# A 31-tap depthwise convolution moved to column tiles of TensorE, and the 256-token x operand laid out in gapless rows at another offset

## The chip, the cores and the metric

The kernel runs on one core of one Trainium2 chip. A core has TensorE (PE, with the weight loads listed apart as PEld), VectorE (DVE), ScalarE (ACT), GpSimd (POOL) and SyncE (SP, which here only issues loads). The metric is the device time of one execution in microseconds (us); lower is better.

## The reference, cut to what matters

Two stacked blocks of layers for one sequence of 256 tokens with model width 1024, all in float32. The first block has four layers (mixers: retention, convolution, dilated attention, retention), each followed by a gated feed-forward layer (hidden 2816); the second puts 16 meta tokens ahead of the 256 (272 tokens) and has a mixer with two branches, a feed-forward layer of 4096, a differential attention and another feed-forward layer. The mixer that the change rewrites is the convolution, layer 1:

```
def _conv_mixer(h, w_in, b_in, w_dw, b_dw, ln_g, ln_b, w_out, b_out):
    a = h @ w_in + b_in
    u = a[..., :D_MODEL] * jax.nn.sigmoid(a[..., D_MODEL:])
    u = lax.conv_general_dilated(              # 31 taps, each channel by itself
        u, w_dw[:, None, :], window_strides=(1,), padding=[(15, 15)],
        dimension_numbers=('NWC', 'WIO', 'NWC'), feature_group_count=D_MODEL) + b_dw
    u = jax.nn.silu(_layernorm(u, ln_g, ln_b))
    return u @ w_out + b_out
```

## The kernel before, in words

Activations lie channels on partitions, tokens along the row: 8 chunks (KD) of 128 channels by 256 tokens (S), or 272 (T2) in the second block. Every float32 value that a large product uses is split in two float32r parts, high and low. The normed input of a layer is the pair `xh`, `xl` (written by `prenorm_chunk`), the hidden of a layer are the pairs `hh`, `hl`, and weights come in quads of 8 blocks of 128x128: SP loads two quads at a time (`raw`, 1 MB), ACT casts the high part (`hi`, 128x1024), DVE subtracts the low part (`lo`). `mmB` (line 322) is one block: three matmuls, hi by xh, hi by xl, lo by xh, with the weights stationary and 256 (or 272) tokens moving. `mmA` (line 331) is the other way round for values that are wanted with tokens on partitions: x is stationary, 512 columns of hi or lo move. `xk` and `xtok` (lines 613 and 616) give the operand slices of x; `kouter` opens a layer with the contraction chunk outside, so that PE can follow chunk by chunk while the norm is still being written.

There is no scheduler behind the kernel: a planner inside it (`Kern.now`, `Engine.cost`, generators in `bg` that `pump` steps between blocks) fixes the order of every queue when the kernel is built, by estimated costs; on the chip each engine runs its queue in that order and waits on semaphores.

The convolution (`conv`, line 1058): 128 blocks of `conv_w_in` give 8 pairs of channel chunks (value and gate); `evac` makes U[c], 128 channels by 256 tokens with 15 zeros at either side. The 31 taps of a chunk are shared out by `TAPS`: the first 13 to 16 go to PE (`taps_pe`: ACT scales the identity by the tap's weights into a 128x128 diagonal `cdg`, and a float32 matmul of U shifted by the tap is accumulated), 121 over all chunks; the other 127 go to DVE (`taps_dve`: scalar_tensor_tensor on 128x256 into two accumulators `cv` and `cacc`). `combine` adds the PE sum to the DVE sum, `stats` builds the layer norm's sums, `act` normalises, and `conv_w_out` follows.

By the allocation of the built program, addresses along a partition are: xh at byte 27392 with 1088 bytes from chunk to chunk, xl at 36096, hi buffers from 72992 in steps of 4096, lo buffers from 101664 in steps of 4096 (a block is 512 bytes); the hh and hl that 256-token products read lie 1024 bytes apart, the first at 136672. Counted from the start of a weight block and modulo 512: xh and xl of chunk k at 480 + 64k, hh and hl at 192, the same for all of them.

Of the kernel before, what the change touches and what calls it, by code (L numbers as in the profile page):

```python
# [19 lines left out]
D = 1024  # L20
# [15 lines left out]
def _vec_layout():  # L36
    n = 0
    for i in range(4):
        for j in range(4):
            VEC[f"n{i}{j}"] = n  # L40
            n += 8
    for name, w in (
        ("mix0", 8), ("mix1", 8), ("mlp0", 8), ("mlp1", 8), ("fin", 8),
        ("cb_in", 16), ("cb_dw", 8), ("cln_g", 8), ("cln_b", 8), ("cb_out", 8),
        ("lconv_w", 32), ("lconv_b", 8), ("lb_r", 8), ("lb_i", 8), ("lam", 8),
        ("mnorm", 8), ("subln", 1), ("cw_dw", 248),
    ):
        VEC[name] = n
        n += w
    return n  # L50
# [13 lines left out]
def shape_consts():  # L64
# [23 lines left out]
    c["amask"] = mk  # L88
    c["cmask"] = np.where(s[None, :] <= s[:, None], 0.0, BIG).astype(f)
# [21 lines left out]
LRU_B = 4  # L111

# [90 lines left out]
class Kern:  # L203
# [212 lines left out]
    def setup(self):  # L416
# [3 lines left out]
        self.xh = cp.tile([128, KD, T2], F32R, name="xh")  # L420
        self.xl = cp.tile([128, KD, T2], F32R, name="xl")
# [142 lines left out]
    def prenorm_chunk(self, c, src, gain, T, perm, have=False):  # L564
# [3 lines left out]
        h, l = view(self.xh[:, c, :T]), view(self.xl[:, c, :T])  # L568
# [54 lines left out]
    def kouter(self, T, outs, key, cut=lambda n: 0):  # L623


        for k in range(KD):
            self.feed(2)
            if k == 0:
                ws = []
                for n, (b, o, first) in enumerate(outs):  # L630
                    w = self.blk(*key(0, n))
                    ws.append(w)
                    self.mm(b[:, o:o + T - cut(n)], w[0], self.xh[:, 0, cut(n):T], first, False)
                for n, (b, o, first) in enumerate(outs):
                    self.mm(b[:, o:o + T - cut(n)], ws[n][1], self.xh[:, 0, cut(n):T], False, False)
                for n, (b, o, first) in enumerate(outs):
                    self.mm(b[:, o:o + T - cut(n)], ws[n][0], self.xl[:, 0, cut(n):T], False, False)
            else:
                for n, (b, o, first) in enumerate(outs):
                    self.mmB(b[:, o:o + T - cut(n)], self.blk(*key(k, n)), self.xtok(k, cut(n), T - cut(n)),  # L640
                             False, k == KD - 1)
# [95 lines left out]
    def boundary(self, perm, gain2, perm2=False, full=False):  # L737
# [39 lines left out]
        if first:  # L777
            self.ve.tensor_tensor(mg, mg, ps[:, :S], ALU.mult)
            o = T - S
            self.ve.tensor_tensor(self.xh[:, 0, o:T], mg, xg, ALU.add)  # L780
            if o:
                self.ve.tensor_scalar(self.xh[:, 0, :o], self.X[:, 0, :o], g, None, ALU.mult)
# [271 lines left out]

    TAPS = (16, 13, 14, 16, 16, 16, 16, 14)
    CD = 1.0

    def conv(self, i, j):
# [8 lines left out]
        ln, U, sums = {}, {}, {}  # L1067
# [5 lines left out]
        def evac(c, b):  # L1073
# [3 lines left out]
            u = self.wk.tile([128, S + 30], F32, name="U", tag="U", bufs=8)  # L1077
# [13 lines left out]
            U[c] = u  # L1091

        def claim():

            for c in range(KD):
                while c not in U:
                    yield None
                for k in range(self.TAPS[c]):
                    d = self.wk.tile([128, 128], F32, name="cdg", tag="cdg", bufs=8)
                    self.sc.activation(d, self.ident, AF.Copy, scale=self.vec("cw_dw", 8 * k + c))  # L1100
                    yield c, k, d

        def taps_pe():
            src, ahead, b = claim(), deque(), None
            more = True
            while more or ahead:
                while more and len(ahead) < 4:
                    x = next(src, 0)
                    if x is None:
                        break  # L1110
                    if x == 0:
                        more = False
                    else:
                        ahead.append(x)
                if not ahead:
                    yield 0.3
                    continue
                c, k, d = ahead.popleft()
                last = k == self.TAPS[c] - 1
                if k == 0:  # L1120
                    b, = yield from self.need(1)
                yield self.w(d, U[c])
                self.mm(b[:, :S], d, U[c][:, k:k + S], k == 0, last)
                if last:
                    sums[c] = b
                    self.spawn(combine(c))
                if k % 2:
                    yield 0.0

        def taps_dve():  # L1130
            for c in range(KD):
                while c not in U:
                    yield 0.3
                shifted = "shift" in done
                if shifted:
                    done.add(("shifted", c))
                acc = [cv[:, c], self.wk.tile([128, S], F32, name="cacc", tag="cacc")]
                for n, k in enumerate(range(self.TAPS[c], 31)):
                    w = self.vec("cw_dw", 8 * k + c)
                    x, a = U[c][:, k:k + S], acc[n % 2]  # L1140
                    if n == 0 and shifted:
                        self.ve.scalar_tensor_tensor(out=a, in0=x, scalar=w, in1=K, op0=ALU.mult, op1=ALU.subtract)
                    elif n == 1 and not shifted:
                        self.ve.tensor_scalar(a, x, w, None, ALU.mult)
                    elif n < 2:
                        self.ve.tensor_scalar(a, x, w, self.vec("cb_dw", c), ALU.mult, ALU.add)
                    else:
                        self.ve.scalar_tensor_tensor(out=a, in0=x, scalar=w, in1=a, op0=ALU.mult, op1=ALU.add)
                    yield self.ve.clock - self.now - 0.5
                self.ve.tensor_tensor(acc[0], acc[0], acc[1], ALU.add)  # L1150
                done.add(c)

        def combine(c):
            while c not in done:
                yield 0.1
            b = sums[c]
            yield self.w(b, cv[:, c]) + (0.0 if c == KD - 1 else self.CD)
            self.ve.tensor_tensor(cv[:, c], cv[:, c], b[:, :S], ALU.add)
# [94 lines left out]
        self.spawn(taps_pe())  # L1253
        self.spawn(taps_dve())
        self.spawn(stats())
        for c in range(3, KD):
# [4 lines left out]
            self.spawn(evac(c, p))  # L1261
        self.until(lambda: len(yk) > 0)
# [613 lines left out]
    def diff(self):  # L1876
# [44 lines left out]
        def project(n):  # L1921
            p = self.bank()
            o = cut(n[0])
            for k in range(KD):
                self.mmB(p[:, :T2 - o], self.blk(*w_in(k, n)), self.xtok(k, o, T2 - o), k == 0, k == KD - 1)
# [169 lines left out]
def pack(inputs):  # L2095
# [20 lines left out]
    for a, b in (("cb_in", "conv_b_in"), ("cb_dw", "conv_b_dw"), ("cln_g", "conv_ln_g"), ("cln_b", "conv_ln_b"),  # L2116
                 ("cb_out", "conv_b_out"), ("cw_dw", "conv_w_dw"), ("lconv_w", "lru_conv_w_2"),
# [3 lines left out]
    c["vec"] = v  # L2121
    row = np.concatenate([f["ret_log1m_decay"].reshape(-1), f["ab_if_bias_2"][0], f["c_lambda_2"][0].reshape(-1)])
# [43 lines left out]
```

## Time and profile before

| | |
|---|---|
| median of 3 runs | 2404.72 us (2403.23 to 2404.73) |
| profiled execution, device time | 2403.58 us |
| its span (first to last instruction) | 2401.7 us |
| PE busy | 2352.9 us, 98% |
| PEld busy | 2242.4 us, 93% |
| DVE busy | 1651.1 us, 69% |
| ACT busy | 1161.6 us, 48% |
| POOL busy | 222.3 us, 9% |

The profile is of one execution. Matmuls are pipelined: the duration of one in the profile reaches past the start of the next, so what a matmul costs in a stream is read from the distance between starts. A float32 matmul (not float32r, and not a transposition by the identity) leaves two records.

### The profile page before, as it was taken

The numbers are of one execution on the slowest core, as the hardware profiler recorded it, in microseconds if no ns is written. First come the engines' busy times: TensorE is split into PE (matmuls) and PEld (weight loads), VectorE is DVE, ScalarE is ACT, GpSimd is POOL, SyncE is SP. The second block draws the span as 40 slices with busy tenths as digits, with TensorE's granted clock in tenths as the row PEclk, the third lists the DMA queues.
The fourth block names the chain that finished last, engine by engine and source line by source line (L and its number), as shares of the span: only waits on it lengthen the run. The fifth ranks groups of instructions, "written<-read, shape, count | busy, mean of one in ns | idle before, by whom it ended". The sixth has DMA issues, their size and how long they took to land.

```text
span 2401.7 us, 43737 instructions
## 1 busy us (share of the span) xinstructions
PE 2352.9 (98%) x18193; PEld 2242.4 (93%) x18193; DVE 1651.1 (69%) x2826; ACT 1161.6 (48%) x1879; POOL 222.3 (9%) x284
## 2 busy tenths in 40 slices
PE   7999999999999999999999999999999999999998
PEld 7889999989998989999998899999999999989998
DVE  7556865898667768876676658566766756586764
ACT  5544544565444454454445444445655434356543
POOL 1002000112002000020020002002000100132000
PEclk9999999999999999999999999999999999999999
DMA  6443553304553544335544444554433445433552
GB/s 237 171 169 131 211 193 141 141 24 155 208 185 137 193 150 141 141 141 193 193 147 182 171 160 172 184 192 159 141 141 139 160 163 190 162 115 114 211 194 106
DMA packets 56935, 387.89 MB, mean 162 GB/s; under 512 B 7360, under 2 KB 8128, under 8 KB 10656
## 3 DMA queue, kind: packets, MB, share of 16 engines
q1 hardware_dynamic: 53280, 381.18, 44.1%
q10 hardware_dynamic: 3200, 2.99, 0.4%
q8 instruction: 143, 2.34, 0.4%
q0 software_dynamic: 256, 0.92, 0.1%
q14 instruction: 56, 0.46, 0.1%
HBM read 384.02 MB, written 1.05 MB: 160 GB/s over the span
## 4 chain that ended last, share of the span: by engine, by line
PE 86%; DVE 6%; POOL 3%; issue 2%; ACT 2%; DMA 1%; SPq 0%; ACTq 0%; DVEq 0%; POOLq 0%
PE b L312 84%; PE b L316 2%; DVE lo L198 2%; POOL X L198 1%; ACT hi L198 1%; POOL acc L198 1%; DVE cv L198 1%; DVE xl L198 1%; DVE cacc L198 1%; POOL rs L198 1%; DVE xh L198 0%; PE b L345 0%; DVE psq L198 0%; DMA raw<-in_w 0%; POOL psq L198 0%
## 5 line engine op out<-in xcount | busy, mean ns | idle before, releaser
L198 DVE TENSOR_TENSOR lo<-raw,hi 128x1024 fp32r<-128x1024 f32 (+1 forms) x723 | 876.7, 1235 | 266.4 <-ACT hi L198 264.8
L312 PE MATMUL b<-xh,hi 128*128 128x256 f32 (+1 forms) x3272 | 937.3, 290 | 14.2 <-ACT hi L198 9.3
L312 PE MATMUL b<-xl,hi 128*128 128x256 f32 (+1 forms) x3272 | 917.3, 284 | 4.3 <-DVE xl L198 4.1
L312 PE MATMUL b<-xh,lo 128*128 128x256 f32 (+1 forms) x3272 | 914.1, 283 | 0.9 <-DVE lo L198 0.9
L198 ACT CAST hi<-raw 128x1024 fp32r<-128x1024 f32 (+1 forms) x723 | 738.5, 1044 | 266.4 <-PE b L312 227.0
L312 PEld LDWEIGHTS b<-xh,hi 128*128 128x128 f32 x3272 | 611.9, 189 | 23.6 <-ACT hi L198 9.5
L312 PEld LDWEIGHTS b<-xl,hi 128*128 128x128 f32 x3272 | 611.8, 188 | 8.9 <-DVE xl L198 6.7
L312 PEld LDWEIGHTS b<-xh,lo 128*128 128x128 f32 x3272 | 614.2, 189 | 1.1 <-DVE lo L198 1.1
L312 PE MATMUL b<-hh,hi 128*128 128x256 f32 (+1 forms) x1792 | 504.1, 281 | 0.6 <-ACT hh L198 0.6
L312 PE MATMUL b<-hl,hi 128*128 128x256 f32 (+1 forms) x1792 | 500.2, 279 | 0.6 <-DVE hl L198 0.4
L312 PE MATMUL b<-hh,lo 128*128 128x256 f32 (+1 forms) x1792 | 500.3, 279 | 0.0
L312 PEld LDWEIGHTS b<-hh,hi 128*128 128x128 f32 x1792 | 336.9, 188 | 2.3 <-issue 0.8
L312 PEld LDWEIGHTS b<-hl,hi 128*128 128x128 f32 x1792 | 336.8, 188 | 2.0 <-DVE hl L198 1.6
L312 PEld LDWEIGHTS b<-hh,lo 128*128 128x128 f32 x1792 | 336.9, 188 | 0.0
L198 DVE TENSOR_TENSOR t<-b,R 128x512 f32<-128x512 f32 x96 | 65.4, 689 | 199.3 <-PE b L312 197.5
L312 PE MATMUL b<-hi,xh 128*128 128x512 f32 x352 | 142.4, 404 | 0.5 <-DVE xh L198 0.5
L312 PE MATMUL b<-lo,xh 128*128 128x512 f32 x352 | 140.0, 398 | 0.3 <-DVE lo L198 0.3
L312 PE MATMUL b<-hi,xl 128*128 128x512 f32 x352 | 139.3, 396 | 0.0
L198 ACT ACTIVATE sg<-t 128x256 f32<-128x256 f32 x88 | 36.6, 419 | 193.3 <-DVE t L198 193.2
L198 POOL TENSOR_TENSOR acc<-acc,sq 128x256 f32<-128x256 f32 (+1 forms) x90 | 83.1, 923 | 385.5 <-ACT sq L198 233.0
L198 POOL TENSOR_TENSOR psq<-psq 128x512 f32<-128x512 f32 x8 | 12.0, 1506 | 973.8 <-ACT psq L198 973.8
L198 ACT ACTIVATE sq<-X 128x256 f32<-128x256 f32 (+1 forms) x91 | 39.7, 439 | 116.8 <-POOL X L198 73.4
(313 smaller groups left out, 2127.9 us busy)
## 6 DMA issues: line engine op xcount, KB each, us to landing
raw<-in_w SPq DMA_DIRECT2D x359, 1024.0 KB, 4.8
raw<-in_w SPq DMA_DIRECT2D x4, 256.0 KB, 6.0
raw<-in_w SPq DMA_DIRECT2D x2, 512.0 KB, 9.7
dp<-in_c_dp SPq DMA_DIRECT2D x2, 512.0 KB, 4.8
wr<-in_lru_w SPq DMA_DIRECT2D x1, 1024.0 KB, 6.8
X<-in_x POOLq DMA_DIRECT2D x1, 640.0 KB, 9.5
c_rcs<-in_c_rcs ACTq DMA_DIRECT2D x2, 256.0 KB, 5.0
c_amask<-in_c_amask ACTq DMA_DIRECT2D x1, 512.0 KB, 3.5
```

The source lines that it names most:

```text
L198: return f(*args, **kw)
L312: self.nc.tensor.matmul(out, lhsT, rhs, start=start, stop=stop, skip_group_check=True)
L316: self.nc.tensor.transpose(out, in_, ident)
```

## The change

Three things are edited. First, the x operand: `xh` and `xl` become flat tiles. A 256-token layer keeps chunk k at element 56 + 256k (bytes 224 + 1024k), a 272-token layer at 272k as before. With `cw_dw` gone from the vector table all that is allocated behind it moves down by 992 bytes together: xh starts at 26400, hi at 72000, hh at 135680. Counted from the start of a weight block and modulo 512, xh and xl of a 256-token layer now lie at 192 for every k; hh and hl stay at 192; the 272-token layout stays where it was against the weights. The differential attention's queries (256 tokens cut out of 272) keep the 272-token layout.

Second, the taps: all 31 (and a 32nd of weight zero) go to PE, and `taps_dve`, `TAPS` and the 121 diagonals are gone. After U[c] is written, ACT's queue issues four DMAs within SBUF that lay each group g of 32 channels out on 128 partitions, 4 shifts of each channel (`cr`, line 1108 of the changed file). POOL multiplies a 32-column selection matrix by the tap weights (`ctw`, 128x1024). Then a chunk is 32 float32 matmuls: 8 steps of 4 taps by 4 channel groups, each with 128 rows, 32 weight columns and 256 tokens, writing 32 PSUM partitions, the four groups in turn.

Third, the order: the taps of chunks 5 and 6 wait in the plan until all of `conv_w_in` is issued, so that they stand ahead of chunk 7's. `combine` only adds the bias (ACT, or DVE with the shift).

```
+    XOFF = 56
+    def xpart(self, t, k, T, t0=0, n=None):
+        a = (self.XOFF if T == S else 0) + k * T + t0
+        return t[:, a:a + (T - t0 if n is None else n)]
     def xk(self, k, T):
-        return self.xh[:, k, :T], self.xl[:, k, :T]
-    def xtok(self, k, t0, n):
-        return self.xh[:, k, t0:t0 + n], self.xl[:, k, t0:t0 + n]
+        return self.xtok(k, 0, T, T)
+    def xtok(self, k, t0, n, T=S):
+        return self.xpart(self.xh, k, T, t0, n), self.xpart(self.xl, k, T, t0, n)
...
-    TAPS = (16, 13, 14, 16, 16, 16, 16, 14)
-    CD = 1.0
+    COPY, TAP = 4.0, 3.5
...
             self.unlock("evac")
-            U[c] = u
+            r = self.wk.tile([128, 4, RW], F32, name="cr", tag="cr", bufs=3)
+            yield self.w(u) - 0.3
+            x = u[:]
+            ps = x.ap[0][0]
+            for g in range(4):
+                nc.scalar.dma_start(out=r[:, g], in_=bass.AP(x.tensor, x.offset + 32 * g * ps, [[ps, 32], [1, 4], [1, RW]]))
+            self.times.write(r, max(self.now, self.times.read(u)) + self.COPY)
+            U[c] = r
...
+        def tapw(c):
+            w = self.wk.tile([128, 32, 32], F32, name="ctw", tag="ctw", bufs=3)
+            self.gp.tensor_tensor(w, m32[:, None, :].to_broadcast([128, 32, 32]),
+                                  cwt[:, 32 * c:32 * c + 32].unsqueeze(2).to_broadcast([128, 32, 32]), ALU.mult)
+            return w
+        def taps():
+            ws = {c: tapw(c) for c in range(2)}
             for c in range(KD):
+                while c not in U or c in (KD - 3, KD - 2) and "in" not in done:
                     yield 0.3
+                yield self.w(U[c], ws[c])
+                b, = yield from self.need(1)
+                w = ws.pop(c)
+                for q in range(8):
+                    for g in range(4):
+                        self.mm(b[32 * g:32 * g + 32, :S], w[:, 4 * q + g], U[c][:, g, 4 * q:4 * q + S], q == 0, q == 7,
+                                TAP / 32)
+                if c + 2 < KD:
+                    ws[c + 2] = tapw(c + 2)
+                self.spawn(combine(c, b))
+                yield 0.0
+        def combine(c, b):
+            yield self.w(b)
+            if "shift" in done:
+                done.add(("shifted", c))
+                self.ve.scalar_tensor_tensor(out=cv[:, c], in0=b[:, :S], scalar=self.vec("cb_dw", c), in1=K,
+                                             op0=ALU.add, op1=ALU.subtract)
+            else:
+                self.sc.activation(cv[:, c], b[:, :S], AF.Identity, bias=self.vec("cb_dw", c))
             self.rel(b)
...
-        self.spawn(taps_pe())
-        self.spawn(taps_dve())
+        self.spawn(taps())
         self.spawn(stats())
```

On PE at the end of the convolution's first product the order before was this (`b<-xh,hi` and its like are blocks of `conv_w_in`, `U,cdg` a tap by a diagonal, the `onesD` rows the layer norm's sums, the `hi` rows matmuls that fill a wait, `hh` the first of `conv_w_out`):

```order
L312 MATMUL b_5188<-U,cdg 128x256 x2
L312 MATMUL b_5353<-U,cdg 128x256 x16
L312 MATMUL b_5425<-U,cdg 128x256 x16
L312 MATMUL b_5497<-U,cdg 128x256 x16
L312 MATMUL b_5569<-U,cdg 128x256 x16
L312 MATMUL b_5640<-U,cdg 128x256 x10
L312 MATMUL b_5683<-onesD,a_5267 128x1 x2
L312 MATMUL b_5683<-onesD,a_5268 128x1 x2
L312 MATMUL b_5640<-U,cdg 128x256 x4
L312 MATMUL b_5683<-onesD,cv 128x1 x2
```

Of the 121 taps 41 stood among the blocks ahead of these rows and 80 stand here, in the order of chunks 2 to 7. The same place on PE in the changed kernel:

```order
L316 MATMUL b_5309<-xh,lo 128x256
L316 MATMUL b_5387<-cr,ctw 32x256 x32
L316 MATMUL b_5429<-cr,ctw 32x256 x32
L316 MATMUL b_5468<-cr,ctw 32x256 x32
L316 MATMUL b_5505<-onesD,a_5203 128x1 x2
L316 MATMUL b_5505<-onesD,a_5204 128x1 x2
L316 MATMUL b_5505<-onesD,cv 128x1 x2
```

Three chunks (5, 6, 7) are left behind the blocks, 32 matmuls each; the other five stand among the blocks in groups of 32.

On ACT's queue in the changed kernel, at the same place (`sg` is the gate's sigmoid, `cr<-U` the four DMA issues of a chunk, `cv<-b` a chunk's combine, `csq` the squares for the norm):

```order
L202 ACTIVATE sg<-t_5317,V 128x256
L202 CAST hi<-raw 128x1024
L1110 DMA cr<-U 128x1x284 x4
L202 ACTIVATE sg<-t_5381,V 128x256
L1110 DMA cr<-U 128x1x284 x4
L202 ACTIVATE csq<-cv 128x256 x3
L202 ACT_TABLE_LOAD
```

Chunk 7's four issues come right behind its sigmoid and wait for DVE's U; nothing but the squares and the norm's table load is queued behind them.

## Rows read from the trace of the kernel before

**Rows 1.** The page: busy times, and the chain that ended last by engine.
```profile
PE 2352.9 (98%) x18193; PEld 2242.4 (93%) x18193; DVE 1651.1 (69%) x2826; ACT 1161.6 (48%) x1879; POOL 222.3 (9%) x284
...
PE 86%; DVE 6%; POOL 3%; issue 2%; ACT 2%; DMA 1%; SPq 0%; ACTq 0%; DVEq 0%; POOLq 0%
```

**Rows 2.** Groups of PE by form: count, busy us, mean ns, idle before, releasers.
```profile
L312 PE MATMUL b<-xh,hi 128*128 128x256 f32 x2496 | 708.2, 287 | 13.0 <-ACT hi L198 9.3 <-DVE xh L198 3.2
...
L312 PE MATMUL b<-hh,hi 128*128 128x256 f32 x1408 | 391.8, 278 | 0.0
...
L312 PE MATMUL b<-hi,xh 128*128 128x512 f32 x352 | 142.4, 404 | 0.5 <-DVE xh L198 0.5
```

**Rows 3.** Timeline of PE, layer 0's feed-forward: start us, us, what.
```profile
301.05 0.28 PE L312 MATMUL b<-xh,hi 128*128 128x256 f32 x1
...
306.74 0.28 PE L312 MATMUL b<-hh,hi 128*128 128x256 f32 x1
...
309.46 0.28 PE L312 MATMUL b<-xh,hi 128*128 128x256 f32 x1
```

**Rows 4.** Timeline of PE in a 272-token feed-forward layer.
```profile
1944.13 0.29 PE L312 MATMUL b<-hh,hi 128*128 128x272 f32 x1
...
1989.53 0.29 PE L312 MATMUL b<-xh,hi 128*128 128x272 f32 x1
...
2031.62 0.29 PE L312 MATMUL b<-hh,hi 128*128 128x272 f32 x1
```

**Rows 5.** Timeline of PE in layer 0's retention, 512 columns moving.
```profile
47.84 0.39 PE L312 MATMUL b<-lo,xh 128*128 128x512 f32 x1
...
60.19 0.39 PE L312 MATMUL b<-hi,xh 128*128 128x512 f32 x1
...
63.69 0.39 PE L312 MATMUL b<-vg,ah 128*128 128x512 f32 x1
...
65.50 0.40 PE L312 MATMUL b<-vg,al 128*128 128x512 f32 x1
```

**Rows 6.** What reads tile U: durations min/median/max, first and last start us.
```profile
L312 PE MATMUL b<-U,cdg x242: 377/378/631, 444.3 to 525.4; 128*128 128x256 f32 x121
L198 DVE SCALAR_TENSOR_TENSOR cv<-U,V,cv x59: 469/475/955, 448.3 to 524.6; 128x256 f32<-128x256 f32 x59
```

**Rows 7.** Convolution by stretch: length; busy PE, PEld, DVE, ACT, POOL; PEclk; DMA.
```profile
414.60:485.40 70.80, 67.28 (x487) 63.77 (x488) 63.34 (x117) 40.59 (x85) 16.57 (x33) 1.00 0.36 129
485.40:526.60 41.20, 38.09 (x171) 31.39 (x169) 40.41 (x92) 23.92 (x79) 8.54 (x10) 0.96 0.02 10
```

**Rows 8.** Timeline of DVE just behind the convolution's first product.
```profile
486.46 0.68 DVE L198 TENSOR_TENSOR t<-b,R 128x512 f32<-128x512 f32 x1
...
488.57 0.48 DVE L198 SCALAR_TENSOR_TENSOR U<-t,V,sg 128x256 f32<-128x256 f32 x1
```

**Rows 9.** Timeline of ACT with its queue's DMA issues (ACTq), two places.
```profile
10.96 0.45 ACTq L413 DMA_DIRECT2D c_ident<-in_c_ident  x1
...
487.18 0.51 ACT L198 ACTIVATE sg<-t,V 128x256 f32<-128x256 f32 x1 [2.34 <-DVE t L198]
```

**Rows 10.** DMA issues by line: count, KB each, median us from issue to landing.
```profile
raw<-in_w SPq DMA_DIRECT2D x359, 1024.0 KB, 4.8
...
out<-fo ACTq DMA_DIRECT2D x2, 256.0 KB, 2.5
```

**Rows 11.** Timeline of PE: float32 matmuls on the whole array and on tiles.
```profile
45.88 1.89 PE L312 MATMUL b<-qk 128*128 128x256 f32 x8
...
831.22 0.28 PE L312 MATMUL b<-xh,lo 128*128 128x256 f32 x1
831.43 1.09 PE L312 MATMUL b<-as,av 128*64 128x128 f32 x16
...
1720.72 1.58 PE L312 MATMUL b<-vt,A 128*16 128x258 f32 x6
```

**Rows 12.** Timeline of POOL in the convolution.
```profile
489.93 0.84 POOL L198 TENSOR_TENSOR a<-a,cv 128x256 f32<-128x256 f32 x1 [7.13 <-DVE cv L198]
```

More of the change, by code (lines that the diff above doesn't have):

```diff
@@ L45, in _vec_layout @@
         ("lconv_w", 32), ("lconv_b", 8), ("lb_r", 8), ("lb_i", 8), ("lam", 8),
-        ("mnorm", 8), ("subln", 1), ("cw_dw", 248),
+        ("mnorm", 8), ("subln", 1),
     ):
@@ L88, in shape_consts @@
     c["amask"] = mk
+    c["m32"] = (s[:, None] // 4 == np.arange(32)[None, :]).astype(f)
     c["cmask"] = np.where(s[None, :] <= s[:, None], 0.0, BIG).astype(f)
@@ L111 @@
 LRU_B = 4
+UW, RW = S + 31, S + 28
 class Bank:
@@ L419, in setup @@
         self.V = cp.tile([128, NV], F32, name="V")
-        self.xh = cp.tile([128, KD, T2], F32R, name="xh")
-        self.xl = cp.tile([128, KD, T2], F32R, name="xl")
+        self.xh = cp.tile([128, KD * T2], F32R, name="xh")
+        self.xl = cp.tile([128, KD * T2], F32R, name="xl")
         self.R = cp.tile([128, T2], F32, name="R")
@@ L567, in prenorm_chunk @@
         view = (lambda a: a.rearrange("p (j i a) -> p j i a", j=4, i=4)) if perm else (lambda a: a)
-        h, l = view(self.xh[:, c, :T]), view(self.xl[:, c, :T])
+        h, l = [view(x) for x in self.xk(c, T)]
         g = self.vec(gain, c)
@@ L779, in boundary @@
             o = T - S
-            self.ve.tensor_tensor(self.xh[:, 0, o:T], mg, xg, ALU.add)
+            self.ve.tensor_tensor(self.xpart(self.xh, 0, T, o), mg, xg, ALU.add)
             if o:
-                self.ve.tensor_scalar(self.xh[:, 0, :o], self.X[:, 0, :o], g, None, ALU.mult)
+                self.ve.tensor_scalar(self.xpart(self.xh, 0, T, 0, o), self.X[:, 0, :o], g, None, ALU.mult)
         self.feeder = feed()
@@ L1066, in conv @@
         self.ve.memset(self.ones256, 1.0 / 256)
-        ln, U, sums = {}, {}, {}
+        m32 = self.const("m32")
+        cwt = self.w1.tile([128, 256], F32, name="cwt")
+        nc.scalar.dma_start(out=cwt, in_=self.ap["cwt"])
+        ln, U = {}, {}
         done = set()
@@ L1076, in evac @@
             t = self.wk.tile([128, 2, S], F32, name="t1", tag="t1")
-            u = self.wk.tile([128, S + 30], F32, name="U", tag="U", bufs=8)
+            u = self.wk.tile([128, UW], F32, name="U", tag="U", bufs=3)
             self.gp.memset(u[:, 0:15], 0.0)
@@ L1090, in evac @@
             self.unlock("evac")
-            U[c] = u
-        def claim():
-            for c in range(KD):
[L1096 to L1115, printed above, removed]
-                    yield 0.3
[L1117 to L1158, printed above, removed]
+            r = self.wk.tile([128, 4, RW], F32, name="cr", tag="cr", bufs=3)
[4 more added lines that the diff above has]
+                nc.scalar.dma_start(out=r[:, g], in_=bass.AP(x.tensor, x.offset + 32 * g * ps, [[ps, 32], [1, 4], [1, RW]]))
@@ L1261, in conv @@
             self.spawn(evac(c, p))
+        done.add("in")
         self.until(lambda: len(yk) > 0)
@@ L1924, in project @@
             for k in range(KD):
[L1925 removed]
+                self.mmB(p[:, :T2 - o], self.blk(*w_in(k, n)), self.xtok(k, o, T2 - o, T2), k == 0, k == KD - 1)
             keep(n, p)
@@ L2121, in pack @@
     c["vec"] = v
+    w = np.zeros((32, D), np.float32)
+    w[:31] = f["conv_w_dw"][0]
+    c["cwt"] = np.ascontiguousarray(w.reshape(8, 4, 8, 4, 32).transpose(4, 1, 2, 0, 3).reshape(128, 256))
     row = np.concatenate([f["ret_log1m_decay"].reshape(-1), f["ab_if_bias_2"][0], f["c_lambda_2"][0].reshape(-1)])
```

11 lines of the change are left out of this document (6 added, 5 removed).

## The prediction, made before the changed kernel was run

> **What bounds the kernel now.** I read the page first: PE is busy 98% of the span and the chain that ended last is 86% PE [rows 1]. So what counts is how fast PE goes from one matmul to the next, and where it has to follow another engine.
>
> For the first I took the groups of PE by form [rows 2]: a 256-column matmul is listed at 278 to 287 ns, but these durations overlap, so the cost is the distance between starts. In the timeline of a feed-forward layer 48 matmuls with x moving stand between 301.05 and 306.74, which is 118.5 ns each, and the 24 with hh or hl moving that follow stand between 306.74 and 309.46, 113.3 ns each [rows 3]. Same columns, weights out of the same buffers, microseconds apart; x costs 5.2 ns more. Two things differ: where x lies against the weights (480 + 64k modulo 512, against a constant 192), and what the matmuls belong to.
>
> For the second I took the convolution by stretch [rows 7]. While `conv_w_in` runs, PE is busy 67.28 of 70.80 us. In the next 41.20 us PE works at taps, but DVE is busy 40.41 of them: 127 of the 248 taps are DVE's and the last starts at 524.6 [rows 6]. That stretch ends when DVE does.
>
> **The x operand.** Rows 2 count 2496 blocks of three 256-column matmuls. Of these, 64 blocks are the differential attention's queries, which keep the old layout; 2432 blocks, 7296 matmuls, move to 192, where hh and hl are. If place decides, each falls from 118.5 to 113.3 ns: 7296 x 5.2 = 37.9 us. At the front of a layer PE waits for x chunks and weights, 13.0 us before the first of a block's three [rows 2]; those waits end when they ended, so some faster blocks only wait longer. I take 2 us off: **36 us**. The ends are 0 (place is not the cause) and 38.
>
> The 1056 matmuls with 512 columns moving (three times the 352 of rows 2) have x as weights. They take (60.19 - 47.84) / 53 = 233 ns; the retention's own, whose operands are at 0 modulo 512 to each other, take (65.50 - 63.69) / 8 = 226 ns [rows 5]. After the change these stand at 320, which no row shows. Between 2 us lost and 1056 x 6.7 ns = 7 us won I take **3 us**, nearer the lower end, since at 272 columns place does not tell: 360 matmuls with hh and hl at all multiples of 64 take 126.1 ns, 336 with x 125.3 [rows 4]. Those 272-column matmuls keep their place and their time.
>
> **The taps.** A float32 matmul of 256 columns on the whole array is two records 216 ns apart, (1.89 - 0.38) / 7, so 0.43 us [rows 11]. Removed are 121 of them: 41 among the blocks (17.7 us) and 80 in the second stretch. Added are 256, each a quarter of the array's columns. Were they to run one by one, a chunk would cost 32 x 0.43 = 13.8 us; four at once, 3.45 us. The nearest row is `as,av`: 64 columns wide, alternating halves, 8 matmuls of 128 columns in 16 records, (1.09 - 0.32) / 7 = 110 ns for one against 216 ns on the whole array, so two halves run at once [rows 11]. Narrowness alone wins nothing: `vt,A`, 16 columns wide and always at one place, takes 240 ns a record [rows 11]. I take four at once, carrying on what the halves do, and keep two at once (6.9 us) and one (13.8 us) as bounds. Going onto tiles costs 0.09 us (the start at 831.43 stands 0.21 behind one that is followed at 0.118 elsewhere) and a first record longer by 0.05; I put 0.23 us to a visit and assume the way back like the way in.
>
> The Trainium skill, "TensorE: Matmul & The Clock Gate", Part 3 (Measured speedup vs the span model), gives 2.38 times for three column tiles of 32. Carried to four as an estimate, 3.2 times, a chunk would be 4.3 us and the kernel 7 us slower than I say; no row here has more than two tiles.
>
> Among the blocks: five groups, 5 x (3.45 + 0.23) = 18.4 us for 17.7, **0.7 us lost**. Behind the blocks: three groups, 10.4 + 0.25 us, then a drain and one DVE pass of some 0.5 us, 11.4 us in place of 41.2: **29.8 us won**. Together 29 us.
>
> **What covers the copies.** Chunk 7 cannot start before its U is made and copied. Its evacuation took from 486.46 to 489.05 between DVE taps that are now gone [rows 8]; by the durations 0.68, 0.51 and 0.48 us it takes some 2.1 us from the last block [rows 8, 9]. Four issues of 0.45 us on ACT follow [rows 9], and a landing, for which the nearest row is the 256 KB that ACT's queue sends in 2.5 us [rows 10]: 6.4 us. Chunks 5 and 6 cover 7.1 us, so it is hidden with 0.7 us to spare; at the 4.8 us of a weight load [rows 10] PE would wait 1.6 us. The earlier chunks have blocks between. Behind the issues ACT has weight casts, which run some four quads ahead of their use. POOL makes eight products of 128x1024, four times the 0.84 us of a 256-column one, 3.4 us [rows 12], 27 us over 80, ahead of use but ahead, too, of the zeroing of U. DVE and ACT lose 127 taps and 121 diagonals; beyond the second stretch that is worth nothing. For two table loads and queueing at the front I add **1 us**.
>
> **Sum.** 36 + 3 + 29 - 1 = 67 us off the profiled execution's 2403.6 us: 2336.6. The median of the runs is 1.1 us above that execution, so I predict 2338 us.
>
> **Rivals.**
> - *Two tiles at once.* Each tile needs its own moving stream, and the halves already take float32 at twice the whole array's rate. Then a chunk is 6.9 us: 5 x 7.1 - 17.7 = 18 lost among the blocks, 21.6 for 41.2 won behind them, 1.6 us in all instead of 29. 2365 us. For it: the rows stop at two. Against: nothing in the two shows a limit.
> - *The place of x is not the cause.* Then 39 us stay and the time is 2377. For it: rows 4, where place tells nothing. Against: rows 3, and that with 256 columns a stream of 1024 bytes ends where the next begins, modulo 512, which a 272-column one does not.
> - *Slower: the tiles run one by one.* 13.8 us a chunk among the blocks, on PE, which is the bound there: 5 x 14.0 - 17.7 = 52.5 lost, and 42.3 for 41.2 behind them. 2421 us. It decides where a chunk takes over 11.9 us, fewer than 1.2 tiles at once, for then the taps give back all that x wins. Against it: `as,av`.
> - *Half of it and no more*, both of the first two: the taps' 1.6 us is left, 2404 us.
>
> The Trainium skill speaks for the second of these: "SBUF — State Buffer" (Who interferes with whom) has PE read its moving operand and its weights through two independent ports and wait for nobody. By that rule the kernel would land at 2377. The trace agrees with it at 272 columns and has 5.2 ns against it at 256.
>
> **How the numbers follow.** Both work: 0.70. Two at once: 0.13. Place not the cause: 0.10. One by one: 0.04. Both halves fail: 0.02; something else that makes it slower, such as PE waiting for copies at every chunk: 0.01. A measurement of this kernel tells about 0.2%, 5 us, from no change. Faster by more than that is 0.93, the same 0.02, slower 0.05. The likeliest case's own range is 2328 to 2349: below, no deduction at the layers' fronts (2), the whole 7 us of the 512-column matmuls (4), no extra cost (1), and up to 3 from the second stretch, where the granted clock was 0.96, so partly at 1.2 instead of 2.4 GHz [rows 7]; above, copies that land late (2) and tiles or x that fall short by a quarter (9). The range of 8 in 10 takes in the two-tile case with 4 us on it, 2328 to 2369, and leaves out the others above.
>
> **What would show it.** In the profile after: x and hh matmuls of 256 columns at the same distance, near 113 ns, and 272-column ones unchanged; four `cr,ctw` starts within a few ns and about 0.43 us from one four to the next; 11 us from the last block of `conv_w_in` to the layer norm's sums; DVE with some 60 us less work. I am wrong on x if its matmuls stay at 118, on the taps if a group of 32 takes 7 us or more, on the copies if PE stands before chunk 7.

## The result, and the profile after

The change took the kernel from 2404.72 to 2373.03 us, a ratio of 0.9867 (95% interval 0.9828 to 0.9906). I had said 2338, so it won 31.7 us where I expected 67, and the time lies above my range of 2328 to 2369. The four runs of the changed kernel fall into two pairs, 2365.8 and 2366.9 against 2379.1 and 2379.4, so the median is a time that no run took. The profiled execution is 2379.14, so the traces differ by 24.4 us of span (2401.7 and 2377.3). Disturbed runs, such as one of 4501 us of the kernel that holds three chunks back, are left out of every median and ratio below.

The page of the changed kernel, the lines that answer to [rows 1], to the second of [rows 2] and to [rows 10]:

```profile
PE 2323.5 (98%) x18463; PEld 2208.8 (93%) x18463; DVE 1597.7 (67%) x2688; ACT 1126.8 (47%) x1762; POOL 237.6 (10%) x292
...
PE 70%; DVE 3%; POOL 3%; issue 2%; ACT 1%; DMA 0%; ACTq 0%; DVEq 0%; POOLq 0%
...
raw<-in_w SPq DMA_DIRECT2D x359, 1024.0 KB, 4.8
cr<-U ACTq DMA_DIRECT2D x32, 142.0 KB, 4.0
```

PE is still what bounds it, and DVE has 53 us less to do. The groups of PE by form (count, busy us, mean ns, idle before):

```profile
L316 PE MATMUL b<-xh,hi 128*128 128x256 f32 x2496 | 697.8, 283 | 13.0 <-ACT hi L202 9.2 <-DVE xh L202 3.3
...
L316 PE MATMUL b<-hh,hi 128*128 128x256 f32 x1408 | 395.7, 281 | 0.0
...
L316 PE MATMUL b<-hi,xh 128*128 128x512 f32 x352 | 140.1, 398 | 0.5 <-DVE xh L202 0.5
L316 PE MATMUL b<-cr,ctw 128*32 128x256 f32 x512 | 35.5, 411 | 6.6 <-DMA cr<-U 4.2 <-issue 2.3
```

x is shorter than before, as forecast, but hh is longer: 281 ns against 278 [rows 2]. I had left hh alone in the sum. The taps wait for copies, 4.2 us by the releasers that the profile names.

**The five long streams.** Four feed-forward layers and the last MLP each have some 1408 matmuls of 256 columns behind each other with no wait, 150 us and more. The view by stretch counts how many run in 150 us of each (length; busy PE, PEld, DVE, ACT, POOL; clock; DMA). Before, in the first of them:

```profile
250.00:400.00 150.00, 150.00 (x1285) 150.00 (x1284) 100.83 (x168) 65.39 (x78) 0.00 (x0) 1.00 0.53 191
```

After, all five:

```profile
250.00:400.00 150.00, 150.00 (x1276) 150.00 (x1275) 99.52 (x161) 63.95 (x76) 0.00 (x0) 1.00 0.54 190
575.00:725.00 150.00, 150.00 (x1276) 150.00 (x1275) 94.91 (x134) 61.23 (x72) 0.00 (x0) 1.00 0.53 190
1050.00:1200.00 150.00, 150.00 (x1326) 150.00 (x1325) 99.87 (x142) 64.10 (x77) 0.00 (x0) 1.00 0.53 186
1450.00:1600.00 150.00, 150.00 (x1276) 150.00 (x1275) 94.80 (x135) 61.32 (x72) 0.00 (x0) 1.00 0.55 196
2205.00:2355.00 150.00, 150.00 (x1276) 150.00 (x1275) 95.60 (x159) 66.57 (x93) 2.24 (x4) 1.00 0.49 176
```

Four count 1276 and one 1326. These are two fixed cadences, a cadence being the distance from start to start: every matmul of such a stream, x and hh alike, takes 117.8 ns in the four and 113.3 ns in the one. Before, x took 118.7 to 118.9 and hh 113.4 to 113.5 on average in each of the five, and 1285 came out here. So in four of five streams hh has lost 4.4 ns a matmul, and x won 0.9 and not 5.2. One stream at 113.3 instead of 117.8 is 1408 x 4.45 ns = 6.3 us. Two of them would be the 13 us between the pairs of runs, which is not shown, since only one execution has a trace. Below I say that a stream draws one of the two.

Over all matmuls of 256 columns that follow each other without a wait, the mean distance of x went from 118.7 to 116.1 ns and that of hh from 113.8 to 116.4: 7296 x 2.6 = 19 us won, 4224 x 2.6 = 11 us lost.

**The convolution** by stretch, against [rows 7]: from its first product to the last block, and on to the layer norm's sums.

```profile
413.64:490.16 76.52, 70.36 (x724) 58.37 (x724) 45.54 (x61) 27.11 (x42) 37.43 (x47) 0.98 0.48 155
490.16:510.28 20.12, 15.89 (x204) 9.76 (x205) 5.15 (x9) 3.44 (x7) 2.87 (x4) 0.92 0.42 126
```

The blocks take 76.5 us where they took 70.8, and the part behind them 20.1 where it took 41.2 and I expected 11.4. From its first matmul to the first of `conv_w_out`, a stretch that I use below, the convolution went from 117.7 to 101.9 us: 15.8 of the 24.4 us. Its taps on PE (start us, us, idle before and what ended it), a group among the blocks and the three behind them:

```profile
458.51 3.66 PE L316 MATMUL b<-cr,ctw 128*32 128x256 f32 x64
...
491.03 5.58 PE L316 MATMUL b<-cr,ctw 128*32 128x256 f32 x68 [0.88 <-DMA cr<-U]
499.97 9.02 PE L316 MATMUL b<-cr,ctw 128*32 128x256 f32 x124 [3.35 <-DMA cr<-U]
```

A chunk is 64 records and takes 3.6 us: four tiles do run at once. But PE stands before chunk 5 and inside chunk 6: the 68 records are chunk 5 and the first four of chunk 6, the 124 are the rest of chunk 6 and chunk 7, which follows without a wait.

### The profile page after: what moved, and what is told of

Same layout as the page of the kernel before. It is cut to its first block, busy times and chain, and to the rows that moved or that the text cites. A ratio compares the mean times of both kernels' runs of the same rounds, so it can differ in the third digit from the quotient of the medians.

```text
span 2377.3 us, 44102 instructions
## 1 busy us (share of the span) xinstructions
PE 2323.5 (98%) x18463; PEld 2208.8 (93%) x18463; DVE 1597.7 (67%) x2688; ACT 1126.8 (47%) x1762; POOL 237.6 (10%) x292
## 3 DMA queue, kind: packets, MB, share of 16 engines
q8 instruction: 145, 2.38, 0.4%
## 4 chain that ended last, share of the span: by engine, by line
PE 70%; DVE 3%; POOL 3%; issue 2%; ACT 1%; DMA 0%; ACTq 0%; DVEq 0%; POOLq 0%
PE b L316 68%; PE b L320 2%; POOL X L202 1%; ACT hi L202 1%; DVE lo L202 1%; POOL acc L202 1%; DVE xl L202 1%; POOL rs L202 0%; PE b L349 0%; DVE psq L202 0%; POOL psq L202 0%; DVE xh L202 0%; DMA cr<-U 0%; DVE ptmp L202 0%; DVE X L202 0%
## 5 line engine op out<-in xcount | busy, mean ns | idle before, releaser
L316 PE MATMUL b<-xh,hi 128*128 128x256 f32 (+1 forms) x3272 | 926.9, 287 | 14.1 <-ACT hi L202 9.2
L316 PEld LDWEIGHTS b<-xh,hi 128*128 128x128 f32 x3272 | 613.8, 189 | 24.4 <-ACT hi L202 9.4
L202 ACT ACTIVATE sq<-X 128x256 f32<-128x256 f32 (+1 forms) x91 | 39.7, 438 | 117.3 <-POOL X L202 73.3
```

Source lines behind the costliest of these rows:

```text
L202: return f(*args, **kw)
L316: self.nc.tensor.matmul(out, lhsT, rhs, start=start, stop=stop, skip_group_check=True)
```

## Experiments

**One part alone.** First the x rows without the taps:

```diff
 (the kernel before)
+    XOFF = 56
+    def xpart(self, t, k, T, t0=0, n=None):
+        a = (self.XOFF if T == S else 0) + k * T + t0
+        return t[:, a:a + (T - t0 if n is None else n)]
...
```

> The x rows of the change alone, the taps as before. My prediction priced this part at 39 us (36 for the 256-column matmuls and 3 for those of 512): 2404.7 - 39 = 2366. Theory A, from the two traces: matmuls of 256 columns run at one of two cadences, 113.3 or 117.8 ns, which a start after a wait or an fp32 piece picks and which then stays until the next break; the gapless rows give the x matmuls the same two values as hh, and whole FFN streams of 1408 matmuls now keep one of them. Then x gains little and jumps from run to run: the profiled after was 24.4 us of span faster, of which the conv stretch held 15.8, so this part is worth about 9: 2396, in steps of about 6 us between runs (1408 x 4.45 ns), none of the mean gaps of a long stream between 114.5 and 117. Theory B, the place sets the cadence by itself and the slow streams of the profiled run are an accident: near 2366 in most runs.

Measured: 2389.2 us, ratio 0.9934 (0.9913 to 0.9955), its runs between 2385.4 and 2395.0. In its trace two of the five streams count 1276 and three 1326, none between; the second and the fourth:

```profile
595.00:745.00 150.00, 150.00 (x1326) 150.00 (x1325) 97.14 (x136) 63.42 (x78) 1.59 (x1) 1.00 0.55 191
...
1460.00:1610.00 150.00, 150.00 (x1276) 150.00 (x1275) 96.11 (x136) 61.56 (x73) 0.00 (x0) 1.00 0.52 189
```

So the same x and hh code draws one of two cadences per stream, and this execution drew better than that of the change. Theory A holds in kind and missed by 7 us in size, since it took one draw for the rule. Theory B would have 1326 everywhere. In this kernel weights and x both lie 992 bytes further on than in the change (224 modulo 256), at the same distance to each other, and both cadences are there: the same distance gave the same pair at two addresses.

Then the taps without the x rows:

```diff
 (the changed kernel)
-        a = (self.XOFF if T == S else 0) + k * T + t0
+        a = k * T2 + t0
```

> The column-tiled taps alone, x rows 272 elements apart for 256 tokens too, as before. My prediction priced the taps at 29 us less 1 of extra cost: 2404.7 - 28 = 2377. From the traces: the conv stretch lost 15.8 us in all, so 2389, with the copies' issue at 0.6 to 0.7 us each on ACT and their landing at about 4 us. Theory A says that the x cadence is then as before, mean gaps of about 118.5 ns and no steps of 6 us between runs.

Measured: 2387.3 us, 0.9922 (0.9905 to 0.9940), all runs within 4 us. The convolution takes 100.6 us; x is at 118.7 and hh at 113.9 as before. 15.3 and 17.2 us add up to 32.5 where the change won 31.7: as far as runs that draw can tell, the two halves do not disturb each other, and each is short of its term.

**The place of x.** Two other constant places:

```diff
-    XOFF = 56
+    XOFF = 24
```

> The change with one number altered: x starts at element 24 and not 56, so x stands 64 bytes past the weights modulo 512 and not 192, while hh stays at 192. Theory A with a switch of place as a break: in the FFN each unit goes from x to hh and back, and in the kernel before hh after such a switch took 113.3 mostly; then both lock anew each time, mostly fast, and the FFN streams come to about 114 to 115 ns: 2350 to 2360. Theory A with only waits and fp32 pieces as breaks: as the change, 2366 to 2380 in steps of 6. Theory B, the place alone: one cadence of x in all streams, not 113.3 if 192 is a good place and 64 is not; the time then says which.

```diff
-    XOFF = 56
+    XOFF = 48
```

> As the run with 24, but x starts at element 48: 160 bytes past the weights modulo 512, one of the eight places that the x rows took in turn in the kernel before, now the same for every row. If it is enough that the place stays the same from matmul to matmul, x locks at 113.3 or 117.8 here too and the time is that of the change or of the run with 24. If places at 32 modulo 64 are the slow ones, x stays at 118 to 119 ns or above, as before, and the time is 2385 to 2390 (the conv's 15.8 us alone).

Measured: 2386.2 us (0.9918, 0.9896 to 0.9939) and 2383.5 us (0.9904, 0.9882 to 0.9926), each about the taps alone. Neither of my numbers for the first came out. At 64 x took 117.8 ns in all five streams; at 160 a repeating pattern of 115 to 120 ns with a mean of 117.3. hh, which stays at 192, came back to 113.3 within a few matmuls after every x stretch at 160, and in four of five streams after x at 64. A constant place is not enough, then, and a step from another place back to 192 seems to bring the 113.3.

Two scans changed the place from sub-layer to sub-layer within one kernel:

```diff
-    XOFF = 56
+    XOFF, XTAB = 56, [8, 120, 40, 120, 72, 120, 88, 104]
...
         self.drain()
+        self.XOFF = self.XTAB[0]
+        self.XTAB = self.XTAB[1:]
```

> The change with the place of x altered from one sub-layer to the next, so that one run shows five places more: past the weights modulo 512, x stands at 0 in the FFN of layer 0, at 128 in that of layer 1, at 256 in layer 2's, at 320 in layer 3's, at 384 in the last MLP, and at 448 in the mixers of layers 1, 2 and 3 (hh stays at 192). Theory A (two cadences, picked at a start, kept until a break): with x at any multiple of 64 every x stretch is at 113.3 or at 117.8 ns and nothing between, and hh comes back to 113.3 after x at least in some streams, as in the run with x at 64, where x itself was at 117.8 in all five streams. If the place decides which of the two x takes, then some place gives 113.3 in the whole stream and is better than 192, where either came; if the draw at the start decides, places other than 64 show both in one trace, by stream. Theory B (only the distance that hh has is good): x at 116 to 119 in all five streams.

The second has `XTAB = [57, 52, 58, 62, 54, 52, 60, 64]`.

> The place of x by sub-layer, close to 192: 196 in layer 0's FFN, 200 in layer 1's, 184 in layer 2's, 208 in layer 3's, 224 in the last MLP; 176 in the mixers of layers 1 and 3, 216 in layer 2's. In the scan by 64 the cadence went with the place modulo 256: 0 and 256 gave 119.7 and 119.6, 64 and 320 117.8 and 117.2, 128 and 384 118.8 and 118.7, 192 and 448 113.3 or 117.8. If 192 is an edge of 64-byte rows, all places within 64 bytes above it read as one or two cadences, and the odd places add a part; if the cadence moves with the distance, 196 and 200 lie close to 192 and take 113.3 or 117.8 too. One of them that gives 113.3 alone would be the place to use.

Mean distance of x matmuls in the long streams, taken from the starts in the traces (place: bytes past the weights; 0 to 384 from the first scan and the two runs above, the rest from the second):

```
place   0    64   128   160   176   184   192           196   200   208   224   256   320   384
ns    119.7 117.8 118.8 117.3 119.2 120.1 113.3 / 117.8 121.6 120.0 119.2 118.3 119.6 117.2 118.7
```

(176 is from the mixers' stretches, the others from a feed-forward layer or the last MLP; 216, in one mixer, gave 120.7.) At 448, in the mixers of the first scan, stretches of x at 113.5 and at 117.8 stood side by side, as at 192. What I had written down as theory A, that any multiple of 64 locks, is refuted; place decides, places 256 bytes apart agree within 0.6 ns, and 192 is a point, not a region: 4 bytes past it x takes 121.6 ns. The runs of hh behind x at 196 took 117.8 and 113.4 in turn. The stream at 196, to be read against the 1276 and 1326 of the change:

```profile
250.00:400.00 150.00, 150.00 (x1255) 150.00 (x1254) 99.67 (x163) 64.56 (x78) 0.00 (x0) 1.00 0.52 185
```

The first scan took 2380.5 us (0.9900, 0.9878 to 0.9921), the second, run once, 2400.3.

**A break on purpose.** If 192 has both cadences, and a step from another place picks the 113.3, one row of eight can do it:

```diff
-        a = (self.XOFF if T == S else 0) + k * T + t0
+        a = (self.XOFF - (8 if k == 0 else 0) if T == S else 0) + k * T + t0
```

> The change with one x row of eight moved: row 0 starts at element 48 (160 bytes past the weights modulo 256), the seven others stay where the change has them (192). So far hh, which stands at 192, came back to 113.5 ns after every x stretch that ended at another place (before, x at 160, the scan), and kept whichever cadence the stream had where x stood at 192 too. Theory A2 (192 has both cadences; a step to another place and back is a break, after which the fast one comes): every unit now starts anew, hh is at 113.5 and x at about 114.3 in all five long streams, which saves (881 x 3.5 + 527 x 4.3) = 5.3 us in each stream that was slow; against the profiled run of the change with four slow streams some 20 us, 2359, and the runs lie within 3 us of each other. Rival: the place that x comes from picks the slow cadence as often as the fast one: x at 113.3 and 117.8 from unit to unit, mean near 115.5: 2366 to 2370. Rival: x is slow after row 0 always: x 117.8, hh 113.5, 2371 to 2375.

Measured: 2362.4 us, 0.9817 (0.9800 to 0.9833), 10.6 us under the change in the medians. The five streams:

```profile
250.00:400.00 150.00, 150.00 (x1320) 150.00 (x1319) 102.18 (x166) 66.43 (x81) 0.00 (x0) 1.00 0.54 192
575.00:725.00 150.00, 150.00 (x1320) 150.00 (x1320) 97.12 (x139) 63.46 (x75) 0.00 (x0) 1.00 0.54 194
1050.00:1200.00 150.00, 150.00 (x1320) 150.00 (x1320) 97.10 (x140) 62.95 (x75) 0.00 (x0) 1.00 0.53 191
1460.00:1600.00 140.00, 140.00 (x1233) 140.00 (x1232) 87.05 (x120) 58.44 (x69) 1.17 (x1) 1.00 0.58 204
2215.00:2355.00 140.00, 140.00 (x1235) 140.00 (x1233) 83.03 (x129) 60.22 (x82) 4.43 (x6) 1.00 0.46 164
```

The draw is gone: x at 114.1 to 114.3 and hh at 113.3 ns in all five. Both rivals are refuted. The two later kernels with this row, below, have all ten of their streams like these; in the traces of the five kernels with every x row at 192, 10 of 25 streams drew 113.3. My 2359 was 3 us low and the runs lie within 7 us, not 3; the profiled one (2366.1, the longest of the four) has a convolution of 106.0 us.

**The copies.** Three kernels aim at the convolution. One issues the copies from SP:

```diff
-                nc.scalar.dma_start(out=r[:, g], in_=bass.AP(...
+                nc.sync.dma_start(out=r[:, g], in_=bass.AP(...
```

> The change with the 32 copies issued by SP and not by ACT. Theory C: what stretches the conv's tail is ACT's time for the issues, 2.6 to 3.0 us for four, which stands ahead of the hi casts and the sigmoids, so that chunk 6's U comes 7.3 us after its block and chunk 7's 5.8 us after its own. Then the sums after the last taps start about 6 us earlier (14 us after the last block and not 20), and the conv stretch from its first block to the first output matmul is about 95 us and not 101.9. Rival D: the landing of the copies (4.0 us in the median, up to 7.6) is what ends the waits: the stretch stays within 2 us of 101.9. Rival E: SP's queue is held by weight loads that wait for their buffers, and the copies sit behind them: no gain, or 1 to 6 us lost.

Measured: 2369.6 us (0.9861, 0.9826 to 0.9896; in the traced execution its long streams drew as those of the change), the convolution 93.0 us, the sums 14.4 us after the last block. Theory C's two numbers came out; rivals D and E did not. Yet the copies also landed sooner, after 3.3 us in the median and not 4.0, so this run does not tell the time of the issues from that of the landings. ACT around the last blocks, first in the changed kernel (ACTq is a DMA issue):

```profile
485.63 2.58 ACTq L1110 DMA_DIRECT2D cr<-U  x4
488.25 1.05 ACT L202 CAST hi<-raw 128x1024 fp32r<-128x1024 f32 x1 [4.92 <-PE b L316]
491.19 0.51 ACT L202 ACTIVATE sg<-t,V 128x256 f32<-128x256 f32 x1 [1.89 <-DVE t L202]
491.60 1.03 ACT L202 CAST hi<-raw 128x1024 fp32r<-128x1024 f32 x1
492.35 2.95 ACTq L1110 DMA_DIRECT2D cr<-U  x4
495.40 0.51 ACT L202 ACTIVATE sg<-t,V 128x256 f32<-128x256 f32 x1 [2.77 <-DMA cr<-U]
496.56 2.91 ACTq L1110 DMA_DIRECT2D cr<-U  x4
```

Four issues hold ACT 2.6 to 3.0 us. Chunk 5's stand ahead of a weight cast at 488.25 (with SP as issuer the cast in this place of the queue starts at 479.29, right behind the one before it); in the same trace the DVE subtraction of those weights waits for it, and the product `t` of chunk 6 stands behind that subtraction on DVE:

```profile
489.33 1.23 DVE L202 TENSOR_TENSOR lo<-raw,hi 128x1024 fp32r<-128x1024 f32 x1 [3.73 <-ACT hi L202]
490.47 0.68 DVE L202 TENSOR_TENSOR t<-b,R 128x512 f32<-128x512 f32 x1
491.79 0.48 DVE L202 SCALAR_TENSOR_TENSOR U<-t,V,sg 128x256 f32<-128x256 f32 x1 [0.63 <-issue]
...
496.00 0.48 DVE L202 SCALAR_TENSOR_TENSOR U<-t,V,sg 128x256 f32<-128x256 f32 x1 [1.51 <-issue]
```

Chunk 6's U is there at 492.3, though its blocks ended at 484.5, and the issues of its copies hold back chunk 7's sigmoid to 495.40 and its U to 496.00. With SP as issuer, ACT in the same place:

```profile
485.14 0.51 ACT L202 ACTIVATE sg<-t,V 128x256 f32<-128x256 f32 x1 [4.81 <-DVE t L202]
485.56 1.03 ACT L202 CAST hi<-raw 128x1024 fp32r<-128x1024 f32 x1
488.54 0.51 ACT L202 ACTIVATE sg<-t,V 128x256 f32<-128x256 f32 x1 [1.95 <-DVE t L202]
```

Chunk 7's sigmoid starts 2.5 us after its last block, not 5.2, and its U is there after 3.6 us, not 6.3. Chunk 6's U still takes 5.6 us, for 7.8.

The second keeps one more chunk back to cover the last copies:

```diff
-                while c not in U or c in (KD - 3, KD - 2) and "in" not in done:
+                while c not in U or c in (KD - 4, KD - 3, KD - 2) and "in" not in done:
...
-            r = self.wk.tile([128, 4, RW], F32, name="cr", tag="cr", bufs=3)
+            r = self.wk.tile([128, 4, RW], F32, name="cr", tag="cr", bufs=4)
```

> The change with the taps of chunk 4 kept back too until the last block is out (and a fourth buffer for the copies), so that three groups of 3.6 us and not two cover the copies of chunk 7. PE is idle 7.3 us of the 18.0 us from the first held group to the end of the last. If only cover is lacking, 3.6 us of them go: conv stretch 98.3 us. If the copies of chunks 6 and 7 are late for a reason that moves with them (ACT's queue), under 1.5 us.

Measured: 2359.8 us, the median of three (0.9823, 0.9801 to 0.9846; two of the five streams of the traced one, which took 2367.9, drew the 113.3), the convolution 96.1 us, 5.8 less than in the change and so more than the 3.6 that cover alone could give. The blocks shrank by more than the group that moved out of them; I did not follow what else went.

The third takes both together with the moved row 0:

> The change with copies on SP, three chunks held back and row 0 of x at element 48, all three. If they add: conv stretch 91 us or less for 101.9 (the copies on SP alone gave 93.0, three held alone 96.1), and the five long streams as in the run with row 0 moved: 2379 - 11 - 20 = 2348. If SP and the held chunks take the same idle time, the conv stretch is 93.

Measured: 2349.5 us, 0.9768 (0.9753 to 0.9782), runs within 2.6 us. Its convolution takes 89.8 us, and behind the blocks PE stands no more:

```profile
478.83 14.14 PE L316 MATMUL b<-cr,ctw 128*32 128x256 f32 x256
492.90 1.05 PE L316 MATMUL b<-onesD,a 128*128 128x1 f32 x8
```

The same stretch in the view by stretch:

```profile
478.85:492.60 13.75, 13.75 (x257) 10.36 (x256) 3.65 (x7) 1.76 (x4) 6.13 (x7) 1.00 0.84 281
```

Four groups in 13.75 us are 3.44 us a chunk, at a granted clock of 1.00.

**272 columns.** Do those lock too, if their rows keep one place? In the first MLP only hh and hl could be given such rows:

```diff
-            hid[u] = self.splitp(s, T)
+            hid[u] = self.splitp(s, T, 320 if T == T2 else T)
```

> The change with the 272-column hh and hl tiles of the first MLP put in rows of 320 elements, so that they all stand at 192 modulo 256 past the weights (before, at 0, 64, 128 and 192 in turn). The 768 matmuls that read them took 126.0 ns in every run. If a constant place is what lets a stream lock, they go to 120 or 124.4 (272 columns at 2.4 GHz are 113.3, and the 256-column ones stand 6.7 or 11.1 ns over their own 106.7): 1 to 5 us less. Rival: 272 columns lock at no place, 126 stays.

The run, once, took 2362.9 us; three of its five long streams had drawn 113.3, so this time says nothing of the rows. Their starts, from the first hh of a run of 384 to the first x behind it, do:

```profile
1907.30 0.29 PE L316 MATMUL b<-hh,hi 128*128 128x272 f32 x1
...
1954.66 0.29 PE L316 MATMUL b<-xh,hi 128*128 128x272 f32 x1
```

47.36 us for 384 are 123.3 ns, where [rows 4] have 126.1; 2.1 us for both runs of hh. It is one more case in which place counts; 272-column x rows were not tried.

All four edits together, row 0 of x, the copies on SP, three chunks held back and these hh rows:

> The three edits of the run before last, and the hh rows of the first MLP at 320 elements: in the run with those rows alone the 768 matmuls that read hh went from 126.0 to 123.3 ns, which is 2.1 us. If it adds: 2349.5 - 2.1 = 2347.4, 57 us under the kernel before, and the runs within 4 us of each other. If the wider rows move the buffers so that other streams change place, 2349 or above.

Measured: 2345.3 us, 0.9754 (0.9741 to 0.9768), runs from 2345.1 to 2348.7. This is the best version: 59.8 us under the kernel before, 27.7 under the change.

## Why the prediction was wrong

**The x operand: mis-sized, because a second half of it was missing.** The step that failed is "If place decides, each falls from 118.5 to 113.3 ns: 7296 x 5.2 = 37.9 us". Place decides, and 192 is the right place; so the rival "the place of x is not the cause" is wrong too. But I read hh's 113.3 in one stretch [rows 3] as the cadence of that place, when it is one of two, 113.3 and 117.8. Before, hh had the faster one nearly always; x, at its eight places, broke the stream before every run of hh, and the run that moved row 0 shows that such a break is enough. With x at 192 too there is no break between them: a stream of 1408 keeps what it began with, and in the profiled run four of five began with 117.8. The x rows alone were worth 15.3 us and not 39, in runs that spread over 10 us with the draw. With the break put back the x matmuls come to a mean of 114.8 ns and hh to 113.9: 7296 x (118.7 - 114.8) = 28 us for the forecast 38, a working from one trace. Of the rest some 4 us are row 0 and the step back (0.9 ns on the 4177 x matmuls of the long streams), the others the shorter stretches of the mixers and layer fronts, where x still has a mean of 115.6 ns.

The rule that I weighed, from the Trainium skill, "SBUF — State Buffer" (Who interferes with whom), is that PE reads its moving operand through a port of its own and waits for nobody. It speaks of engines in each other's way; I stretched it to a place that costs nothing, and that does not hold: 113.3 ns at 192 and 121.6 ns 4 bytes further, the same shape and clock. That rival's 2377, and the two-tile rival's 2365, lie as near to the runs as they do by chance.

**512 columns: right.** `hi,xh` went from 404 to 398 ns a piece, and the distance between starts over the three kinds from a mean of 233.2 to 229.1 ns: 1056 x 4.1 = 4.3 us for the 3 forecast. **272 columns: right**, 125.3 ns for x and 125.8 for hh, unchanged.

**The taps on PE: right.** Four tiles run at once: 3.44 us for 32 matmuls where PE did not wait, 3.45 forecast. "Two tiles at once" and "one by one" are refuted. My 3.2 times for four tiles, an estimate carried on from the 2.38 times that the Trainium skill has for three column tiles ("TensorE: Matmul & The Clock Gate", Part 3, Measured speedup vs the span model), is low for this shape: 32 x 0.43 = 13.8 us over 3.59 us is 3.8 times. No run here has three tiles.

**The copies: wrong, and this is where the taps' 29 us went to 17.** The failed sentences are "Four issues of 0.45 us on ACT follow", "so it is hidden with 0.7 us to spare" and "Behind the issues ACT has weight casts, which run some four quads ahead of their use". An issue of a copy took 0.62 us in the median and up to 1.5, the landing 4.0 us where I took 2.5. Worse, I counted the issues only on the way of the chunk that they belong to. They also stand ahead of the weight casts and sigmoids of the next, and through the casts ahead of DVE's `t`. So chunk 6's U came 7.8 us after its blocks and the last chunk's 6.3, not 2.1, and PE waited 0.9 us before chunk 5 and 3.4 us inside chunk 6; it did not stand before chunk 7, where I had looked for it. The landing has its own share. The copy that ended the wait inside chunk 6 was issued at 493.59 and landed at 499.93, and PE stood 2.4 us before the first group until that chunk's first copy landed at 450.95, 7.6 us after its issue. What made those landings long was not tested; the DMA engines were 0.71 and 0.98 busy in the two waits. With the issues on SP the convolution gained 8.9 us: 3.6 among the blocks, where the wait before the first group was gone, and 5.8 behind them, with 0.5 lost later. With one more chunk held as well, no wait was left behind the blocks, and the convolution came to 89.8 us, 27.9 less than before. That is the 28 of my sum only nearly, for some 1.6 us of it belong to x (384 matmuls, 118.4 ns before, 114.3 there).

**A term I did not have:** what a wait can cost behind its end. The stretches of the wait before the first group, that group, and the one behind it; then the wait inside chunk 6 and what follows it:

```profile
448.60:451.04 2.44, 0.10 (x1) 0.03 (x1) 0.00 (x0) 0.00 (x0) 0.00 (x0) 1.00 0.71 217
451.04:457.28 6.24, 6.24 (x65) 2.99 (x65) 3.32 (x2) 1.55 (x2) 2.12 (x5) 0.73 0.75 165
458.51:462.10 3.59, 3.59 (x66) 1.98 (x65) 0.64 (x1) 1.04 (x1) 0.84 (x1) 1.00 0.88 270
...
496.60:499.97 3.37, 0.01 (x1) 0.00 (x1) 0.28 (x1) 0.42 (x1) 0.72 (x1) 1.00 0.98 365
499.97:505.40 5.43, 5.43 (x69) 3.17 (x73) 0.00 (x0) 0.00 (x0) 0.72 (x1) 0.69 0.27 78
```

A mean granted clock of 0.73 means that for part of the 6.24 us PE had the lower of its two levels, 1.2 instead of 2.4 GHz; the group took 2.65 us longer than the next. The clock is 0.27 x 6.24 = 1.7 us of this. The rest is about what the group's other three copies needed to land, at 451.19, 451.56 and 451.98. A wait of this length does not always bring the clock down: the kernel that holds three chunks back stood 2.38 us in the same place, its clock stayed at 1.00, and its first group took 4.7 us. Behind the wait inside chunk 6 the clock fell again, to a mean of 0.69. The wait itself and the 2.65 us are 5 of the 5.7 us by which the blocks' stretch grew; I had forecast 0.7.

**The range** ended at 2369 because it held the tiles' rival and nothing for hh or for late copies: I moved x onto hh's place and never asked whether hh would stay what it was. Two of the four runs lie in the range all the same; that is luck and no merit of the sum.

## What to carry to other kernels

When two kinds of the same instruction differ in cadence, look at how the numbers are spread over the whole trace, stream by stream, before taking the better one as the price of its cause: two fixed values with nothing between are a state that can change for both. A change that makes one operand like another may take from the other what it had. And count a DMA issue on the engine that issues it, against everything that stands behind it there and against whoever waits for that; SP had the time that ACT did not.

## What the runs showed of the hardware that was not expected

- A stream of 256-column float32r matmuls with its weights 192 bytes (modulo 256) before its moving operand runs at 113.3 or at 117.8 ns a matmul and keeps it for 1408 matmuls; a step to 160 and back brought 113.3 in every long stream of four kernels. At 14 other places tried x took 117.2 to 121.6 ns. After x at 64, hh kept 117.8 in one stream of five, and after x at 200 in the one stream there was, so the place that it comes from seems to count. What picks the cadence after a wait, and why place matters at all, stays open: no run changed how a stream begins.
- Four column tiles of 32, float32, reading four different weights and four different streams: 3.44 to 3.59 us for 32 matmuls of 256 columns, which is 3.8 to 4.0 times the whole array.
- A copy within SBUF of 142 KB: 0.55 to 1.5 us of the issuing engine on ACT and 4.0 us to land in the median, 7.6 us at most; issued by SP the median landing was 3.3 us, single ones up to 8.6.
